# A transformer block on one core: four orders of instructions, and the square of the hidden layer in one VectorE instruction

## The chip, the cores and the metric

The kernel runs on one core of one Trainium2 chip. A core has TensorE (PE; its weight loads are PEld), VectorE (DVE), ScalarE (ACT), GpSimd (POOL), and SyncE (SP), which here issues nearly all DMAs. The metric is the device time of one execution in microseconds (us), the median over runs. The profile is one execution seen by the hardware profiler.

## The reference

```python
def reference(x, norm1_g, w_in, sinks_a, rel_bias_b, out_norm_a_g, out_norm_b_g,
              w_out, norm2_g, w_ff1, w_ff2, final_norm_g):
    n = rms_norm(x, norm1_g)                       # x: 1024 rows x 1024
    qa, ka, va, qb, kb, vb = split(n @ w_in)       # 64 per head
    ya = mixer_a(qa, ka, va, sinks_a)              # 8 heads, 2 of keys; window, ALiBi, sinks
    yb = mixer_b(qb, kb, vb, rel_bias_b)           # 8 heads; own chunk of 64 and 8 before
    y = concat(rms_norm(ya, out_norm_a_g), rms_norm(yb, out_norm_b_g))
    h = x + y @ w_out
    n = rms_norm(h, norm2_g)
    u = square(relu(n @ w_ff1))                    # 1024 x 4096
    h = h + u @ w_ff2
    return rms_norm(h, final_norm_g)
```

Everything is float32, and the kernel keeps about that accuracy.

## The kernel before

Every matrix is used as a sum of a high and a low part, and a product is three matmuls (high by high, high by low, low by high; `mm3`). A split is two instructions: ScalarE rounds to the high part, and VectorE or GpSimd subtracts it from the whole for the low part (`split` at L1395 and L1397 or L1399; `split_y` at L914 and L917 for the attention's outputs).

The first 430 us hold the input projection, the two attentions and the output projection. Matmuls of the projections are filled in between those of the attention. The names the change touches: `values_b` copies one half of the last value projection `vB3` out of its PSUM bank into `ts_vB` (L433), and at the second half takes its maximum (L438). `UnitB.end` joins two parts of a head's output into `Y` (L907, L908). `split_ya` splits a quarter `y` of group A's outputs, which `load_ya` (L947) reads back from DRAM. `out_proj_a` multiplies the quarters q = 0 to 3 with the weights, for each block `tb` of 128 rows and each half `dh` of the 1024 columns, into a bank `op_A`; ScalarE evacuates it to `o` (L1064) and GpSimd adds it to `h`. The row maximum of the scores `S_B` is taken in L620 and L622.

The MLP's products are made by a Strassen scheme of seven products of half size. In ff1 a column group n = 0 to 7 (512 columns of `w_ff1`) runs the products p = 1, 5, 6, 3, 7, 2, 4. Their left operands `X` come from n by transposes (`turned`) and sums (`second_half` for the blocks 1,1 and 1,0: `F` on ScalarE, L1301, and `S` on VectorE, L1304 and L1305; `combined`, `operand`). The right ones, `W`, come from four weight blocks `w`, which ScalarE scales by a power of two found from their maximum (`scaled1`, L1362), then sums `T` on VectorE (L1369), then the split. `product1` runs the matmuls `f`, and evacuates a bank to `kept[p]` (L1447, p = 1, 5, 6) or adds a bank to what is kept and takes the maximum (L1457, p = 3, 7, 2). ScalarE then rectifies with the scale `down1[n]` and squares (L1458, L1459), and `put` stores u in DRAM as `ud`. After p = 4 four more sums on VectorE give the other operands. Also in ff1, `look2` loads each block of `w_ff2` as `m` (512 KB), and ScalarE squares it with a sum (`see_squares`, L1176), from which the scale of that block's group follows.

In ff2, `fetch2` loads a `u` back, `prepare2` scales it by `uup[g]` and splits it to `U` (L1393 to L1399), forms the weight operand `Z` and splits it to `V`; `product2` runs the matmuls (`f_a`, `f_b`, `f_c`), and `add_up` adds them to `C` (L1711).

A framework orders each engine's instructions by a simulated schedule and places the semaphores. TensorE's order is kept as written. A `NoSync` dependency (`add_manual_dep`) orders two instructions of one engine without a wait, and `InOrder` keeps the DMAs of SP in the order in which they were put in. So the order of VectorE and ScalarE can move at places that the diff doesn't name.

Of the kernel before, what the change touches and what calls it, by code (L numbers as in the profile page):

```python
# [53 lines left out]
PAD = 32  # L54
# [4 lines left out]
def kernel(  # L59
# [364 lines left out]

    def values_b(acc, name, dst, t):
# [7 lines left out]
        nc.vector.tensor_tensor(st[:, t], acc, R1[:, t * HALF : (t + 1) * HALF], ALU.mult)  # L433
# [603 lines left out]
    def out_proj_a():  # L1037
# [6 lines left out]
        for tb in range(TB):  # L1044
# [6 lines left out]
            for n in range(8):  # L1051
                q, dh = (n // 2, n % 2) if tb == 0 else (n % 4, n // 4)
# [242 lines left out]
    def second_half(n, g):  # L1295

        if g not in S:
            F[2, g] = page([P, 2, HALF], f"F2{g}", F32)
# [2 lines left out]
        nc.scalar.activation(a22, turned(1, 1, n, g), AF.Copy)  # L1301
# [3 lines left out]
        dve.tensor_tensor(s3, a11, a21, ALU.subtract)  # L1305
# [40 lines left out]
    def scale1(n):  # L1346
# [3 lines left out]
        down1[n] = power(scale_tile("down1", str(n), 3), e, 1.0, -W_UP)  # L1350
# [3 lines left out]
    to_scale1 = {}  # L1354

    def scaled1(n, *blocks):
        up1, left = to_scale1[n]
        for b in blocks:
            if b in left:
                left.remove(b)  # L1360
                w = w1s[(n, *b)]
                nc.scalar.activation(w, w, AF.Copy, scale=up1)  # L1362
# [26 lines left out]
    def split(full, name, engine, alloc, up=None):  # L1389
# [5 lines left out]
        nc.scalar.activation(w[0], full, AF.Copy, scale=1.0 if up is None else up)  # L1395
# [24 lines left out]
    def product1(n, p):  # L1420
# [32 lines left out]
        if p == 4:  # L1453
            nc.scalar.activation(v, ps, AF.Relu, scale=down1[n])
            dve.tensor_reduce(top, ps, mybir.AxisListType.X, ALU.max)
        else:
# [1 line left out]
            nc.scalar.activation(v, v, AF.Relu, scale=down1[n])  # L1458
        nc.scalar.activation(v, v, AF.Square)  # L1459
# [17 lines left out]
        nc.vector.tensor_tensor(col, col, down1.pop(n), ALU.mult)  # L1477
# [117 lines left out]
    def scale_of_u(g, spread=True):  # L1595
# [3 lines left out]
        uup[g] = power(scale_tile("uup", str(g), 4), e, -2.0, 381 + U_UP)  # L1599
# [14 lines left out]
    def prepare2(at):  # L1614
        if at >= len(order2) or order2[at][1:] in ready2:
# [9 lines left out]
            split(a, f"U{n}_{p}", dve if p == 5 else pool, high, uup[g]), split(b, f"V{n}_{p}", dve, high, up2[g])  # L1625
# [42 lines left out]
    for i in range(LOAD2 - 2, LOAD2):  # L1668
# [249 lines left out]
```

## Time and profile before

| | us |
|---|---|
| median of 3 runs | 1038.84 (1038.01 to 1040.87) |
| the profiled execution | 1040.53 |
| its span in the profile | 1038.7 |
| busy in it: PE, DVE, ACT, POOL | 1000.8, 742.5, 692.6, 443.9 |

An engine's busy time is a share of the span; where it idles, the profile names the instruction that released it. TensorE's clock can be lowered; the profile gives the granted share. In rows of the timeline there stand the start, the length of the group, the engine, the source line, the operation, output and inputs, shape, count, and in brackets the idle time ahead of it with what ended it.

### The profile page before, as it was taken

Reading aid. Unit: us, or ns where it says so; the run is one execution under the profiler, and the core shown is the slowest. Engines: PE = TensorE matmul, PEld = TensorE weight load, DVE = VectorE, ACT = ScalarE, POOL = GpSimd, SP = SyncE. Lnnn points to the kernel's source line nnn. Section 1 sums busy time; section 2 is a strip of 40 time slices with the busy share of each in tenths; the row PEclk is TensorE's granted clock in tenths of the full one; section 3 lists DMA queues with packets and bytes.
Section 4 is the critical chain, followed back from the end, with each engine's and each line's share of the span. In section 5 each row is a group of like instructions: output and inputs, shape, how many; then the busy total and the mean of one; then the engine's idle time right before and its main releaser. Section 6 shows DMA issues by size and latency. Waiting matters only on the chain.

```text
span 1038.7 us, 14057 instructions
## 1 busy us (share of the span) xinstructions
PE 1000.8 (96%) x4818; PEld 591.8 (57%) x4818; DVE 742.5 (71%) x1259; ACT 692.6 (67%) x1102; POOL 443.9 (43%) x341
## 2 busy tenths in 40 slices
PE   9999999999979999899999999999899999999997
PEld 7878887777757678544444444444344444444443
DVE  6566777867586748994676667664798776786776
ACT  8666766667577736675867865964777765567346
POOL 0456665242453562105245425434255343345333
PEclk9999999999989999989999999999999999999999
DMA  9944438999999885105678668648699545433004
GB/s 353 254 133 133 129 82 184 194 209 225 209 257 251 207 261 182 62 21 166 211 282 293 205 210 274 195 170 310 257 329 388 189 150 186 159 121 122 1 1 162
DMA packets 150567, 200.63 MB, mean 193 GB/s; under 512 B 78688, under 2 KB 96224, under 8 KB 150496
## 3 DMA queue, kind: packets, MB, share of 16 engines
q1 hardware_dynamic: 150352, 199.47, 63.6%
q8 instruction: 38, 0.62, 0.3%
q14 instruction: 33, 0.27, 0.1%
q10 hardware_dynamic: 144, 0.26, 0.1%
HBM read 120.01 MB, written 42.99 MB: 157 GB/s over the span
## 4 chain that ended last, share of the span: by engine, by line
PE 34%; ACT 8%; issue 7%; DMA 7%; DVE 6%; POOL 2%; SPq 1%; DVEq 0%; POOLq 0%; ACTq 0%
PE f_a L171 13%; PE f_c L171 7%; PE f L171 6%; PE f_b L171 4%; DMA w<-in_w_ff_dram 3%; PE op_B L171 2%; ACT w L1362 2%; DMA m<-in_w_ff_dram 2%; DMA u<-ud 2%; POOL W L1397 2%; ACT k L1459 1%; ACT k L1458 1%; ACT W L1395 1%; DMA G_B<-H_B 1%; ACT m L1176 1%
## 5 line engine op out<-in xcount | busy, mean ns | idle before, releaser
L171 PE MATMUL f<-X,W 128*128 128x512 f16 x1344 | 295.3, 381 | 6.6 <-POOL W L1397 5.0
L171 PEld LDWEIGHTS <-U 128*128 128x128 f16 x1356 | 133.0, 98 | 163.9 <-issue 7.2
L171 PEld LDWEIGHTS <-W 128*128 128x128 f16 x1344 | 131.4, 98 | 166.3 <-POOL W L1397 8.2
L1397 POOL TENSOR_TENSOR U<-u,U 128x1024 f16<-128x1024 f32 x48 | 117.3, 2454 | 170.5 <-ACT U L1395 155.2
L171 PE MATMUL f_a<-V,U 128*128 128x512 f16 x756 | 165.3, 379 | 1.0 <-DVE C L1711 1.0
L1397 POOL TENSOR_TENSOR W<-T,W 128x1024 f16<-128x1024 f32 x29 | 69.7, 2407 | 84.3 <-ACT W L1395 84.3
L1397 POOL TENSOR_TENSOR W<-w,W 128x1024 f16<-128x1024 f32 x21 | 51.6, 2458 | 98.6 <-ACT W L1395 98.6
L171 PE MATMUL f_c<-V,U 128*128 128x512 f16 x384 | 86.0, 384 | 3.5 <-DVE V L1399 2.2
L1393 ACT ACTIVATE u<-u,uup 128x1024 f32<-128x1024 f32 x48 | 53.9, 1141 | 53.1 <-DMA u<-ud 53.0
L1399 DVE SCALAR_TENSOR_TENSOR V<-Z,up,V 128x1024 f16<-128x1024 f32 x32 | 51.3, 1605 | 28.7 <-ACT V L1395 20.7
L1395 ACT ACTIVATE U<-u 128x1024 f16<-128x1024 f32 x48 | 50.2, 1046 | 28.1 <-DVE Z L1369 10.4
L623 ACT ACTIVATE P_B<-P_B,nm_B 128x640 f32<-128x640 f32 (+2 forms) x64 | 44.2, 691 | 32.2 <-DVE nm_B L620 16.6
L171 PE MATMUL op_A<-w_o,y 128*128 128x512 f32 x192 | 58.0, 428 | 4.1 <-DVE ts_vB L433 3.9
L868 DVE SCALAR_TENSOR_TENSOR H_B<-P_B,rc_B,H_B 128x640 f16<-128x640 f32 (+2 forms) x64 | 51.0, 825 | 13.6 <-ACT H_B L863 13.3
L1399 DVE SCALAR_TENSOR_TENSOR V<-w,up,V 128x1024 f16<-128x1024 f32 x24 | 42.2, 1756 | 18.0 <-ACT V L1395 13.8
L171 PE MATMUL ip_qB<-nT,w_qB 128*128 128x512 f32 x192 | 53.7, 406 | 1.1 <-DVE t_kB L407 1.0
L171 PE MATMUL ip_kB<-nT,w_kB 128*128 128x512 f32 x192 | 53.7, 405 | 0.0
L1457 DVE CUSTOM_DVE_ANT_0 k<-f,k 128x1024 f32<-128x1024 f32 x24 | 29.3, 1220 | 31.3 <-PE f L171 22.4
L171 PE MATMUL ip_vB<-nT,w_vB 128*128 128x512 f32 x192 | 51.3, 400 | 0.0
L1395 ACT ACTIVATE V<-Z,up 128x1024 f16<-128x1024 f32 x32 | 36.4, 1138 | 22.2 <-DVE Z L1369 19.3
L171 PE MATMUL ip_qA<-nT,w_qA 128*128 128x512 f32 x192 | 50.7, 398 | 0.3 <-DVE VA L177 0.3
L863 ACT ACTIVATE H_B<-P_B,rc_B 128x640 f16<-128x640 f32 (+2 forms) x64 | 40.8, 685 | 9.5 <-DVE rc_B L860 4.2
(284 smaller groups left out, 1980.1 us busy)
## 6 DMA issues: line engine op xcount, KB each, us to landing
w<-in_w_ff_dram SPq DMA_DIRECT2D x64, 512.0 KB, 7.5
u<-ud SPq DMA_DIRECT2D x56, 512.0 KB, 5.4
ud<-k SPq DMA_DIRECT2D x48, 512.0 KB, 3.1
m<-in_w_ff_dram SPq DMA_DIRECT2D x32, 512.0 KB, 5.8
KkB<-t_kB SPq DMA_DIRECT2D x32, 256.0 KB, 5.0
xr<-in_x_dram SPq DMA_DIRECT2D x8, 512.0 KB, 8.8
st_o<-in_w_out_dram SPq DMA_DIRECT2D x8, 512.0 KB, 4.8
h<-in_x_dram SPq DMA_DIRECT2D x8, 512.0 KB, 4.9
```

The lines of the kernel that those rows point to most:

```text
L171: pe(nc.tensor.matmul(*args, **kw))
L623: nc.scalar.activation(pr, pr, AF.Exp, bias=nm, scale=-1.0, accum_out=sm)
L863: nc.scalar.activation(hi, q, AF.Copy, scale=rc)
L868: nc.vector.scalar_tensor_tensor(lo, q, rc, hi, ALU.mult, ALU.subtract)
L1176: nc.scalar.activation(src, src, AF.Square, accum_out=self.column())
L1362: nc.scalar.activation(w, w, AF.Copy, scale=up1)
L1393: nc.scalar.activation(full, full, AF.Copy, scale=up)
L1395: nc.scalar.activation(w[0], full, AF.Copy, scale=1.0 if up is None else up)
L1397: engine.tensor_tensor(w[1], full, w[0], ALU.subtract)
L1399: engine.scalar_tensor_tensor(w[1], full, up, w[0], ALU.mult, ALU.subtract)
L1457: dve.tensor_tensor_reduce(v, ps, v, 1.0, 0.0, ALU.add, ALU.max, top)
L1458: nc.scalar.activation(v, v, AF.Relu, scale=down1[n])
```

## The change

1. `FIRST_BLOCK`: in `out_proj_a`, the first block of rows alternates the two column halves of the quarters 0 and 1.
2. `behind_values`: the low parts of y and the sum in `UnitB.end` are ordered behind the copy of `vB3`'s second half on VectorE, once that is made.
3. `second_half` is cut in two steps, and between the transposes of `F` and of `S` six matmuls are put.
4. `last_w`: a scale of a weight block is ordered behind the last high part that was split.
5. For p = 3, 7 and 2, VectorE rectifies and squares in one instruction, max(v, 0) times v, in place of ScalarE's two; the scale `down1[n]` no longer enters there. For p = 4 ScalarE keeps both, without the scale. Instead `uup` is now made for each n, as the scale of the group times `down1[n]` squared, and enters where u is split in ff2.
6. `look2` starts one product earlier and leaves out other loads; from `fetch2` one u more is loaded in the last group at p = 6; four operands instead of two are prepared in ff1.
7. `PAD` and the pool of `all` move tiles in SBUF.

```diff
+FIRST_BLOCK = ((0, 0), (1, 0), (0, 1), (1, 1), (2, 0), (2, 1), (3, 0), (3, 1))
-PAD = 32
+PAD = 96
...
+    def behind_values(ins):
+        if freed:
+            dep = mybir.DependencyInfo(mybir.DependencyClass.NoSync, mybir.DependencyReason.DATA)
+            tc.add_manual_dep(ins.ins, freed[0], dep, reason="program order")
...
-        nc.vector.tensor_tensor(st[:, t], acc, R1[:, t * HALF : (t + 1) * HALF], ALU.mult)
+        ins = nc.vector.tensor_tensor(st[:, t], acc, R1[:, t * HALF : (t + 1) * HALF], ALU.mult)
+        if (name, t) == ("vB3", 1):
+            freed.append(ins.ins.name)
...
-            nc.vector.tensor_tensor(y, self.av[:HD], y, ALU.add)
+            behind_values(nc.vector.tensor_tensor(y, self.av[:HD], y, ALU.add))
...
-        split_y(y, f(y[:, 1]), ogc[:, m : m + 1])
+        behind_values(split_y(y, f(y[:, 1]), ogc[:, m : m + 1]))
...
-                q, dh = (n // 2, n % 2) if tb == 0 else (n % 4, n // 4)
+                q, dh = FIRST_BLOCK[n] if tb == 0 else (n % 4, n // 4)
...
-            self.all = small.tile([P, P], F32, tag="all", bufs=1, name=f"all_{self.name}")
+            self.all = fp.tile([P, P], F32, tag="all", bufs=1, name=f"all_{self.name}")
...
-                nc.scalar.activation(w, w, AF.Copy, scale=up1)
+                ins = nc.scalar.activation(w, w, AF.Copy, scale=up1)
+                if last_w:
+                    dep = mybir.DependencyInfo(mybir.DependencyClass.NoSync, mybir.DependencyReason.DATA)
+                    tc.add_manual_dep(ins.ins, last_w[0], dep, reason="program order")
...
-        nc.scalar.activation(w[0], full, AF.Copy, scale=1.0 if up is None else up)
+        last_w[:] = [nc.scalar.activation(w[0], full, AF.Copy, scale=1.0 if up is None else up).ins.name]
...
-            nc.scalar.activation(v, ps, AF.Relu, scale=down1[n])
+            nc.scalar.activation(v, ps, AF.Relu)
+            nc.scalar.activation(v, v, AF.Square)
...
-            nc.scalar.activation(v, v, AF.Relu, scale=down1[n])
-        nc.scalar.activation(v, v, AF.Square)
+            dve.scalar_tensor_tensor(v, v, 0.0, v, ALU.max, ALU.mult)
...
-        steps((second_half, 1, g))
-        steps()
+        steps((last_part, 1, g))
+        steps((third_part, 1, g))
...
-        uup[g] = power(scale_tile("uup", str(g), 4), e, -2.0, 381 + U_UP)
+        up = power(scale_tile("uup", str(g), 2), e, -2.0, 381 + U_UP)
+        for n in range(g * GQ, (g + 1) * GQ):
+            uup[n] = scale_tile("uupn", str(n), NQ)
+            down = down1.pop(n)
+            nc.vector.tensor_scalar(uup[n], up, down, down, ALU.mult, ALU.mult)
...
-        if at > 7:
-            look2(at, p != 1)
+        if at > 6:
+            look2(at, n < 2 or p not in (1, 5))
...
-                for i in range(LOAD2 - 2):
+                for i in range(LOAD2 - 1):
                     fetch2(i)
-            if p in (7, 2):
-                prepare2({7: 0, 2: 1}[p])
+            for i in {7: (0,), 2: (1, 2, 3)}.get(p, ()):
+                prepare2(i)
```

VectorE's order where `vB3`'s second half is copied (H_B are attention weights, P_B and nm_B the scores and their negative row maximum), before:

```order
L917 SCALAR_TENSOR_TENSOR y_2_3405<-y_2_3405,ogc 128x512
L868 SCALAR_TENSOR_TENSOR H_B_1_1_3490<-P_B_1_0_3458,rc_B_1_3455,H_B_1_1_3490 128x640
L868 SCALAR_TENSOR_TENSOR H_B_1_1_3490<-P_B_1_1_3482,rc_B_1_3455,H_B_1_1_3490 128x640
L620 ISA P_B_1_3_3538,nm_B_1_3453<-S_B_1_3_3537,b_B_587 128x640
L620 ISA nm_B_1_3453 128x1
L917 SCALAR_TENSOR_TENSOR y_3_3407<-y_3_3407,ogc 128x512
L908 TENSOR_TENSOR Y_0_3472<-av_B_0_3494,Y_0_3472 64x512
L433 TENSOR_TENSOR ts_vB_3399<-ip_vB_1_3548,R_180 128x512
L622 ISA P_B_0_0_3612,nm_B_0_3607<-S_B_0_0_3611,b_B_586 128x128
```

and now:

```order
L879 SCALAR_TENSOR_TENSOR H_B_1_1_3490<-P_B_1_0_3458,rc_B_1_3455,H_B_1_1_3490 128x640
L879 SCALAR_TENSOR_TENSOR H_B_1_1_3490<-P_B_1_1_3482,rc_B_1_3455,H_B_1_1_3490 128x640
L631 ISA P_B_1_3_3538,nm_B_1_3453<-S_B_1_3_3537,b_B_587 128x640
L631 ISA nm_B_1_3453 128x1
L442 TENSOR_TENSOR ts_vB_3399<-ip_vB_1_3548,R_180 128x512
L928 SCALAR_TENSOR_TENSOR y_2_3405<-y_2_3405,ogc 128x512
L919 TENSOR_TENSOR Y_0_3472<-av_B_0_3494,Y_0_3472 64x512
L928 SCALAR_TENSOR_TENSOR y_3_3407<-y_3_3407,ogc 128x512
L449 TENSOR_REDUCE top_vB_3580<-ts_vB_3399 128x1
L633 ISA P_B_0_0_3612,nm_B_0_3607<-S_B_0_0_3611,b_B_586 128x128
```

The copy has moved ahead of y_2, y_3 and the sum Y, and these with the maximum top_vB stand ahead of the next row maximum.

ScalarE's order some 20 us later (o_1 is the evacuation of op_A_1, y_0 and y_1 the first splits of the second half's quarter), before:

```order
L623 ACTIVATE P_B_0_1_3764,sm_B_0_3737<-P_B_0_1_3764,nm_B_0_3736 128x256
L1064 ACTIVATE o_1_3776<-op_A_1_3756,rgA 128x512
L623 ACTIVATE P_B_0_2_3783,sm_B_0_3737<-P_B_0_2_3783,nm_B_0_3736 128x384
L863 ACTIVATE H_B_0_1_3769<-P_B_0_0_3741,rc_B_0_3738 128x128
L863 ACTIVATE H_B_0_1_3769<-P_B_0_1_3764,rc_B_0_3738 128x256
L623 ACTIVATE P_B_0_3_3811,sm_B_0_3737<-P_B_0_3_3811,nm_B_0_3736 128x512
L914 ACTIVATE y_0_3704<-y_0_3704,ogc 128x512
L1064 ACTIVATE o_0_3827<-op_A_0_3797,rgA 128x512
L914 ACTIVATE y_1_3706<-y_1_3706,ogc 128x512
```

and now:

```order
L634 ACTIVATE P_B_0_1_3764,sm_B_0_3737<-P_B_0_1_3764,nm_B_0_3736 128x256
L634 ACTIVATE P_B_0_2_3783,sm_B_0_3737<-P_B_0_2_3783,nm_B_0_3736 128x384
L874 ACTIVATE H_B_0_1_3769<-P_B_0_0_3741,rc_B_0_3738 128x128
L874 ACTIVATE H_B_0_1_3769<-P_B_0_1_3764,rc_B_0_3738 128x256
L925 ACTIVATE y_0_3704<-y_0_3704,ogc 128x512
L925 ACTIVATE y_1_3706<-y_1_3706,ogc 128x512
L1076 ACTIVATE o_1_3776<-op_A_1_3756,rgA 128x512
L634 ACTIVATE P_B_0_3_3811,sm_B_0_3737<-P_B_0_3_3811,nm_B_0_3736 128x512
```

The evacuation o_1 has moved behind y_0 and y_1.

ScalarE's order ahead of the first split of group 5 in ff1 (w_5_.. are the weight blocks of the group, m_.. the blocks of w_ff2), before:

```order
L1176 ACTIVATE m_5_00_6185,tops_w_2_6084<-m_5_00_6185 128x1024
L1458 ACTIVATE k_6_6117<-k_6_6117,down_4_5917 128x1024
L1459 ACTIVATE k_6_6117<-k_6_6117 128x1024
L1458 ACTIVATE k_5_6082<-k_5_6082,down_4_5917 128x1024
L1362 ACTIVATE w_5_00_6006<-w_5_00_6006,up_5_6227 128x1024
L1362 ACTIVATE w_5_01_6008<-w_5_01_6008,up_5_6227 128x1024
L1362 ACTIVATE w_5_11_6012<-w_5_11_6012,up_5_6227 128x1024
L1362 ACTIVATE w_5_10_6010<-w_5_10_6010,up_5_6227 128x1024
L1459 ACTIVATE k_5_6082<-k_5_6082 128x1024
L1176 ACTIVATE m_5_01_6233,tops_w_2_6084<-m_5_01_6233 128x1024
L1395 ACTIVATE W_1_6237<-w_5_00_6006 128x1024
```

and now:

```order
L1188 ACTIVATE m_4_01_6107,tops_w_2_6105<-m_4_01_6107 128x1024
L1188 ACTIVATE m_4_11_6175,tops_w_2_6105<-m_4_11_6175 128x1024
L1188 ACTIVATE m_4_10_6221,tops_w_2_6105<-m_4_10_6221 128x1024
L1381 ACTIVATE w_5_00_5995<-w_5_00_5995,up_5_6216 128x1024
L1381 ACTIVATE w_5_01_5997<-w_5_01_5997,up_5_6216 128x1024
L1417 ACTIVATE W_1_6225<-w_5_00_5995 128x1024
L1381 ACTIVATE w_5_11_6001<-w_5_11_6001,up_5_6216 128x1024
L1188 ACTIVATE m_5_00_6257,tops_w_2_6105<-m_5_00_6257 128x1024
L1417 ACTIVATE W_5_6262<-T_5_6260 128x1024
```

The rectify and square instructions are gone from it, two scales have moved behind the split of W_1, and the block m_4_10 has moved up to it.

More of the change, by code (lines that the diff above doesn't have):

```diff
@@ L423, in keys_b @@
                         nc.sync.dma_start(f(dst[2 * hl + s][rep * HD : (rep + 1) * HD]), src)
+    freed = []
+    def behind_values(ins):
+        if freed:
+            dep = mybir.DependencyInfo(mybir.DependencyClass.NoSync, mybir.DependencyReason.DATA)
+            tc.add_manual_dep(ins.ins, freed[0], dep, reason="program order")
     def values_b(acc, name, dst, t):
@@ L1295, in second_half, with last_part @@
     def second_half(n, g):
+        last_part(n, g)
+        third_part(n, g)
+    def last_part(n, g):
         if g not in S:
@@ L1299, in second_half, with third_part @@
             S[g] = [(page if g else page2)([P, 2, HALF], f"S{i}_{g}", F32) for i in range(4)]
+        nc.scalar.activation(F[2, g][:, :, part(n)], turned(1, 1, n, g), AF.Copy)
+    def third_part(n, g):
         a11, _, a22 = (F[d, g][:, :, part(n)] for d in range(3))
-        nc.scalar.activation(a22, turned(1, 1, n, g), AF.Copy)
         a21 = turned(1, 0, n, g)
@@ L1349, in scale1 @@
         up1 = power(scale_tile("up1", str(n), 2), e, -1.0, 254 + W_UP)
-        down1[n] = power(scale_tile("down1", str(n), 3), e, 1.0, -W_UP)
+        down1[n] = power(scale_tile("down1", str(n), 5), e, 1.0, -W_UP)
         nc.vector.tensor_tensor(down1[n], down1[n], xdown, ALU.mult)
         to_scale1[n] = up1, [(0, 0), (0, 1), (1, 1), (1, 0)]
-    to_scale1 = {}
+    to_scale1, last_w = {}, []
     def scaled1(n, *blocks):
@@ L1476, in product1 @@
         nc.vector.tensor_reduce(col, top, mybir.AxisListType.X, ALU.max)
-        nc.vector.tensor_tensor(col, col, down1.pop(n), ALU.mult)
+        nc.vector.tensor_tensor(col, col, down1[n], ALU.mult)
         if n % GQ == GQ - 1:
@@ L1624, in prepare2 @@
         ops2[n, p] = (
-            split(a, f"U{n}_{p}", dve if p == 5 else pool, high, uup[g]), split(b, f"V{n}_{p}", dve, high, up2[g])
+            split(a, f"U{n}_{p}", dve if p == 5 else pool, high, uup[n]), split(b, f"V{n}_{p}", dve, high, up2[g])
         )
@@ L1666, in load_acc @@
             queue[0].dma_start(acc[i, j, n], hB[2 * i + n][:, :, j * HALF : (j + 1) * HALF])
-    for i in range(LOAD2 - 2, LOAD2):
+    for i in range(LOAD2 - 1, LOAD2):
         fetch2(i)
```

## The prediction

> **What bounds the kernel now.** I read the first part of the page, then TensorE's table of waits, a table of stretches, and the timeline around each wait.
>
> ```profile
> PE 1000.8 (96%) x4818; PEld 591.8 (57%) x4818; DVE 742.5 (71%) x1259; ACT 692.6 (67%) x1102; POOL 443.9 (43%) x341
> ```
>
> TensorE is busy for 1000.8 of 1038.7 us, and the change takes no matmul away. So at most the 37.9 us in which TensorE idles can be won, and what it loses at a lowered clock. The waits (us in total, times, longest) that concern the change are these:
>
> ```profile
> PE f L171 <- POOL W L1397: 5.0, 4, 1.6
> PE op_A L171 <- DVE ts_vB L433: 3.9, 1, 3.9
> PE S_B L171 <- DVE nm_B L620: 3.7, 4, 1.7
> PE f_c L171 <- DVE V L1399: 2.2, 1, 2.2
> PE tp L174 <- ACT F L1301: 2.0, 1, 2.0
> PE tp L174 <- DVE S L1305: 1.9, 1, 1.9
> PE f L171 <- ACT W L1395: 1.5, 2, 0.8
> PE f_c L171 <- ACT V L1395: 1.2, 1, 1.2
> ...
> 300.00:312.00 12.00, 8.09 (x29) 6.08 (x28) 10.27 (x23) 9.14 (x18) 8.97 (x13) 0.72 1.04 271
> 440.00:450.00 10.00, 8.06 (x30) 3.74 (x29) 10.00 (x16) 5.30 (x8) 0.00 (x0) 0.66 0.00 1
> 575.00:625.00 50.00, 46.70 (x218) 20.91 (x216) 31.59 (x50) 39.08 (x47) 21.07 (x9) 1.00 0.65 213
> 747.00:755.00 8.00, 5.34 (x17) 1.99 (x17) 8.00 (x7) 4.55 (x5) 2.17 (x1) 0.79 1.03 408
> 755.00:1000.00 245.00, 245.00 (x1137) 111.06 (x1136) 189.00 (x140) 149.78 (x144) 106.42 (x43) 1.00 0.49 171
> ```
>
> The stretches give busy us of PE, PEld, DVE, ACT and POOL, then the granted clock. Four places stand out, each the target of one edit: A (300 to 312), B (440 to 450), C (the start of a new column group in ff1, clock 1.00) and D (747 to 755). At A, B and D the clock falls below 1, so a wait there costs more than its own length. From 755 on TensorE never pauses, so an earlier start at D moves the end one for one.
>
> **Place A: the values copy, and what is then behind it.**
>
> ```profile
> 302.54 0.84 DVE L917 SCALAR_TENSOR_TENSOR y<-y,ogc 128x512 fp32r<-128x512 f32 x1
> 304.38 0.69 DVE L433 TENSOR_TENSOR ts_vB<-ip_vB,R 128x512 f32<-128x512 f32 x1
> 305.13 2.93 PE L171 MATMUL op_A<-w_o,y 128*128 128x512 f32 x6 [3.92 <-DVE ts_vB L433]
> ...
> 322.75 0.67 ACT L1064 ACTIVATE o<-op_A,rgA 128x512 f32<-128x512 f32 x1
> 323.27 2.33 SPq L947 DMA_DIRECT2D y<-ya  x4
> 327.26 1.05 PE L171 MATMUL op_A<-w_o,y 128*128 128x512 f32 x3
> 328.58 0.72 ACT L914 ACTIVATE y<-y,ogc 128x512 fp32r<-128x512 f32 x1 [0.93 <-DMA y<-ya]
> ```
>
> TensorE waits 3.92 us for the copy that empties the bank of vB3, and its next six matmuls take 2.93 us where three at 327.26 take 1.05: another 0.8 us, and by the mean clock of 0.72 more after them; I call it 1.4, in all 5.3. With the new order the copy takes the place of the first y behind the row maximum L620, so it runs from 302.54 to 303.24 instead of 304.38 to 305.07, 1.8 us earlier, and FIRST_BLOCK puts three matmuls that don't need that bank (1.05) ahead of those that do. That alone would leave a wait of 3.92-1.83-1.05 = 1.0 us at full clock, a gain of about 4.3. But two low parts y (0.84 each), the sum Y and the reduction of the copied tile are now ahead of the row maxima L622 that release the next two score blocks; DVE has only 12.00-10.27 = 1.7 us free there. I take about 1.4 us as what TensorE keeps.
>
> The order of after shows a new wait behind it. ScalarE's evacuation o_1 (322.75, 0.67) now stands behind y_0 and y_1 of the next quarter, which wait for their load: 323.27 to 328.58, 5.3 us from issue. The load goes out earlier by about the 1 us that TensorE and its queue gain, so y_0 and y_1 end near 327.6+2x0.72 = 329.0, and o_1 at 329.7 instead of 323.42. TensorE needs that bank at 327.26 less 1.4 = 325.9: a wait of 3.8, about as long as the one that was removed, and likely to lower the clock as that one did (half of 2.4 is taken). Of it, about 1.3 us of the longest later wait of the scores on L620 (1.7 of its 3.7 us) is filled. Sum for A: -1.4+3.8+1.2-1.3 = **+2.3**; bounds -5.3 (all goes, nothing comes) and +6.2 (nothing kept, all of the new wait and 2.4 of clock).
>
> **Place B: transposes of block 1,1.**
>
> ```profile
> 430.00 4.27 ACT L1362 ACTIVATE w<-w,up 128x1024 f32<-128x1024 f32 x4 [0.60 <-DVE up L1154]
> 439.78 0.66 PE L174 MATMUL tp<-ident,n 128*128 128x128 f32 x4 [1.98 <-ACT F L1301]
> 442.37 1.09 PE L174 MATMUL tp<-ident,n 128*128 128x128 f32 x4 [1.94 <-DVE S L1305]
> 443.25 8.94 PE L171 MATMUL f<-X,W 128*128 128x512 f16 x31
> ```
>
> Two waits, 1.98+1.94; the transposes behind the second take 1.09 instead of 0.66, and 31 matmuls 8.94 us where 103 take 22.41 (a row below), 0.288 each against 0.218: 2.2. In all 6.5. The new order of the scales takes two of the four L1362 (half of 4.27) from ahead of the evacuation F, so the first wait goes; the twelve matmuls put between the transposes cover some of the second. But DVE is busy for 10.00 of 10.00 us here, and gets the first new square (about 1.3) ahead of the low part of the operand X_4815 that the seventh next product needs. Counting DVE's rows through in the new order, that operand is ready about 1.3 us earlier than now, where a full cover would need 6.5. I take **-1.3**; bounds -5.0 and +0.9 (the square beside a POOL instruction, below).
>
> **Place C: ScalarE's queue in ff1.** Group 5 stands for groups 2 to 6:
>
> ```profile
> 614.43 4.25 ACT L1362 ACTIVATE w<-w,up 128x1024 f32<-128x1024 f32 x4
> 619.54 1.04 ACT L1176 ACTIVATE m<-m 128x1024 f32<-128x1024 f32 x1
> 620.58 1.04 ACT L1395 ACTIVATE W<-w 128x1024 f16<-128x1024 f32 x1
> 621.69 2.12 POOL L1397 TENSOR_TENSOR W<-w,W 128x1024 f16<-128x1024 f32 x1 [13.02 <-ACT W L1395]
> 623.87 22.41 PE L171 MATMUL f<-X,W 128*128 128x512 f16 x103 [1.60 <-POOL W L1397]
> ...
> m<-in_w_ff_dram SPq DMA_DIRECT2D x32, 512.0 KB, 5.8
>   DMA m<-in_w_ff_dram: 12.7, 13
> ...
> L1458 ACT ACTIVATE k<-k,down x24: 1132/1134/1149, 449.4 to 735.2; 128x1024 f32<-128x1024 f32 x24
> L1459 ACT ACTIVATE k<-k x24: 1039/1045/1058, 450.6 to 736.3; 128x1024 f32<-128x1024 f32 x24
> L1256 DVE SCALAR_TENSOR_TENSOR n<-h,r_n,g2b x8: 1283/1284/2160, 391.3 to 430.1; 128x1024 f32<-128x1024 f32 x8
> ```
>
> The first product of a group waits for the high and low part of W_1, 0.8 and 1.6 us each time; over the phase 5.0+1.5 = 6.5. ScalarE runs four scales, a square and an m sum before the split. The change removes 24 x 1.134 + 24 x 1.045 = 52.3 us from ScalarE, and puts two of the scales behind the split. Then the split needs only m, two scales and itself. But m is loaded (5.8 us), and SP issues that load behind a store of u which now follows VectorE's new instruction; 13 of the 32 m sums already wait for their load, 12.7 us. With the load landing near 614.6 the high part ends at 614.6+1.04+2x1.06+1.04 = 618.8 instead of 621.6, and POOL's part at 620.9 instead of 623.8: 2.9 earlier, more than the 2.4 of waits, with 0.5 to spare. For group 2 the same count, with an estimate of 504.3 for its load, gives a wait about 1.3 longer than the 0.9 of now (part of the 1.5 in the table). Sum: -(6.5-0.9)+1.3 = **-4.3**; bounds -6.5 and 0.
>
> VectorE gets 24 instructions over 1024 elements, the nearest of which took 1.28 (L1256) and at most 2.16: 31 to 52 us, less 0 on the path, since in 575 to 625 it was busy for 31.59 of 50 and gets some 6 more. The eight small scale products stand in that slack too. Merging down twice into the scale of U changes a scalar operand alone.
>
> One price hangs on the neighbour:
>
> ```profile
> 734.29 2.14 POOL L1397 TENSOR_TENSOR U<-u,U 128x1024 f16<-128x1024 f32 x1 [1.84 <-ACT U L1395]
> 735.35 2.17 DVE L1399 SCALAR_TENSOR_TENSOR V<-w,up,V 128x1024 f16<-128x1024 f32 x1 [0.67 <-issue]
> ```
>
> An instruction of that kind that starts during a POOL instruction runs on until 1.09 us after its end, 0.9 longer than the 1.28 above. With POOL busy for 21.07 of 50 us, that costs the 24 squares about 10 us of VectorE's slack, and nothing of the path while the low part of W_1 has its 0.5 us. The Trainium skill, SBUF — State Buffer, section "SBUF: two separate sides", says that VectorE with two SBUF inputs and GpSimd take turns on a shared port pair, whoever starts first keeping it for the whole instruction, which speaks against moving a square onto VectorE, since v is both of its inputs. By that rule a square could also hold back POOL's split of W_1 by its full 1.28 us; at five groups, less the 0.5 to spare, the sum below would be up to 3.9 higher. The row agrees for VectorE; no row shows POOL held.
>
> **Place D: the first u of ff2.**
>
> ```profile
> 737.78 1.25 SPq L152 DMA_DIRECT2D u<-ud  x2
> 744.14 1.15 ACT L1393 ACTIVATE u<-u,uup 128x1024 f32<-128x1024 f32 x1 [4.67 <-DMA u<-ud]
> 750.04 7.24 PE L171 MATMUL f_c<-V,U 128*128 128x512 f16 x25 [2.24 <-DVE V L1399]
> ```
>
> Waits of 1.2+2.24, and 25 matmuls at 0.290 instead of 0.218: 1.8. In all 5.2. The second of the two loads goes out some 19 us earlier (at p=6, ahead of the last group's stores), and the V operands are prepared a product earlier (1, 2, 3 at p=2), so both waits go. What is late next is the accumulator C and V_6, about 0.8. **-4.5**; bounds -5.2 and -2.
>
> **Elsewhere.** PAD moves tiles in memory alone, and the tile all changes pool; nothing waits for either in the rows above, and TensorE's order differs only at A, at the transposes and at three small ones. 0.
>
> **Sum.** +2.3-1.3-4.3-4.5 = -7.8. The profiled execution took 1040.53, 1.7 above the median of 1038.84, so 1032.7 for one like it and **1031** for the median.
>
> **Rivals.**
> 1. Every wait goes, and nothing takes its place: 5.3+6.5+6.5+5.2 = 23.5, so 1015. For it: the four edits hit the four places with a lowered clock or repeated waits. Against: o_1 behind a load at A, and DVE's 10.00 of 10.00 at B. With one of A and B it would be about 1023. Together 0.17.
> 2. No change, 1038 to 1041: A at its upper bound (+6.2), B at +0.9, and C and D at -3 and -4. For it: the new wait at A. 0.15.
> 3. Slower: the m load sets C. At each of the seven new groups W_1's high part on ScalarE is behind an m sum, whose load SP issues behind a store that waits for VectorE. If loads land 3.7 us later than I count, each of seven groups waits 3.7-0.5 = 3.2 us, 22 us where 6.5 stood, so C is +16 and the time 1051; from 2 us later on (7 x 1.5 = 10.5, C +4.0) with the rest as forecast the time is 1039, and from 2.5 us on (14, C +7.5) it is 1043, slower by over 0.3%. For it: 13 waits for such loads now, and fewer other instructions ahead to hide them. Against: median landing of 5.8, no DMA of ff1 above it, 0.65 of DMA share. 0.10.
>
> **Chances.** 0.3% of this time, 3.1 us, is about what a measurement can tell from no change. My forecast, 1024 to 1035.7, has 0.58; it, with rival 1, gives faster 0.75, rival 2 same 0.15, rival 3 slower 0.10. The range goes from between rival 1's two times, 1019, to 1039.5, past most of rival 2: that leaves out about 0.08 below and 0.12 above.
>
> **What would show it.** A: ts_vB right behind L620, no wait near 305 above 1.6 us, but an op_A at about 326 waiting 3 to 4 us for ACT's o; if not, A is -4 and I am too high. B: no wait at 439.8, one of 2 to 3 us for X about 8 us later. C: no f waiting for W from group 3 on; one of about 2.2 at group 2; ScalarE waiting for m. VectorE's squares between 1.28 and 2.2. D: no wait of f_c at 747; a C wait under 1.5. Wrong would be a long wait for W in each group, or a TensorE pause after 755.

## The result, and the profile after

| | before | after |
|---|---|---|
| median of 4 runs each | 1039.47 (1038.01 to 1040.87) | 1055.85 (1054.87 to 1057.68) |
| the profiled execution, its span | 1040.53, 1038.7 | 1057.68, 1055.9 |

The changed kernel takes 1.0158 times the time before [1.0145, 1.0172], 16.4 us more. The prediction had 1031 with a range up to 1039.5: its sign was wrong. Two executions of the kernel before, measured beside `e5` to `e8` below, ran at a granted clock of 0.75 and 0.65 and took 1276 and 1670 us; they are left out of the medians and ratios.

The first part of the page of after (the profile of the changed kernel):

```profile
PE 1002.7 (95%) x4818; PEld 591.7 (56%) x4818; DVE 795.5 (75%) x1291; ACT 644.7 (61%) x1054; POOL 448.0 (42%) x341
```

TensorE's work has hardly grown (1002.7 against 1000.8), so 15.3 of the 17.2 us by which the span grew are idle time. VectorE gained 53 us of work and ScalarE lost 48, near what was counted (31 to 52, and 52). TensorE's table of waits of after (us in total, times, longest):

```profile
PE f L172 <- POOL W L1419: 5.8, 6, 1.9
PE f_c L172 <- ACT U L1417: 4.7, 1, 4.7
PE op_A L172 <- ACT o L1076: 4.0, 1, 4.0
...
PE f_a L172 <- DVE topf L1480: 2.6, 1, 2.6
PE f_c L172 <- DVE C L1737: 2.4, 1, 2.4
PE f L172 <- ACT W L1417: 2.3, 2, 1.8
```

The waits for W were to vanish and are longer (5.8+2.3 against 5.0+1.5). New are one for o (forecast) and those of 4.7, 2.6 and 2.4 at and behind the start of ff2 (not forecast).

Where the time was lost is best read from the start of the same matmul in two traces, counted through TensorE's order. The lag is after minus before, in us. In ff2 the 756 matmuls f_a are counted:

| up to | lag | place's own part | forecast |
|---|---|---|---|
| the end of the attention (A) | +3.0 | +3.0 | +2.3 |
| the end of the transposes (B) | +1.7 | -1.3 | -1.3 |
| ahead of column group 7 | -0.05 | -1.75 | |
| the first matmul of ff2 | +5.2 | +5.25 (with the row above C: +3.5) | C: -4.3 |
| f_a matmul 150, at 815.7; lost by 785 (D) | +11.1 | +5.9 | -4.5 |
| f_a matmul 755, the last; lost at 993 | +15.3 | +4.2 | 0 |
| the end of the span | +17.2 | +1.9 | 0 |

**A and B** came by the mechanism worked out. The timeline of after at A:

```profile
303.98 1.65 PE L172 MATMUL op_A<-w_o,y 128*128 128x512 f32 x3 [2.26 <-DVE ts_vB L442]
...
329.23 0.72 ACT L925 ACTIVATE y<-y,ogc 128x512 fp32r<-128x512 f32 x1 [3.86 <-DMA y<-ya]
330.82 0.67 ACT L1076 ACTIVATE o<-op_A,rgA 128x512 f32<-128x512 f32 x1
331.55 1.65 PE L172 MATMUL op_A<-w_o,y 128*128 128x512 f32 x3 [4.04 <-ACT o L1076]
```

The wait for ts_vB fell from 3.92 to 2.26, and o, now behind a y that waits 3.86 for its load, makes a new one of 4.04; 3.8 was forecast. At B the wait for F is gone, that for S stays, and the forecast one for X has come:

```profile
455.06 5.12 PE L172 MATMUL f<-X,W 128*128 128x512 f16 x23 [2.69 <-DVE X L1297]
```

**C.** ScalarE and TensorE of after ahead of group 5, against the rows of before from 614.43 on:

```profile
613.63 1.06 ACT L1188 ACTIVATE m<-m 128x1024 f32<-128x1024 f32 x1 [3.41 <-DMA m<-in_w_ff_dram]
614.91 1.06 ACT L1188 ACTIVATE m<-m 128x1024 f32<-128x1024 f32 x1
618.93 1.06 ACT L1188 ACTIVATE m<-m 128x1024 f32<-128x1024 f32 x1 [2.87 <-DMA m<-in_w_ff_dram]
619.99 2.17 ACT L1381 ACTIVATE w<-w,up 128x1024 f32<-128x1024 f32 x2
622.07 1.04 ACT L1417 ACTIVATE W<-w 128x1024 f16<-128x1024 f32 x1
...
625.47 9.88 PE L172 MATMUL f<-X,W 128*128 128x512 f16 x45 [1.25 <-POOL W L1419]
```

Three m sums stand ahead of the scales, and the third waits for its load until 618.93; I had it at 614.6. The high part ends at 623.1 instead of the counted 618.8. ScalarE is idle for loads most of that time: over the phase its waits for m (from the view of the m line) grew from 12.7 us in 13 to this:

```profile
  DMA m<-in_w_ff_dram: 39.2, 12
```

Group 5 still starts with no longer a wait than before (1.25 against 1.60); group 7 does not. The timeline there:

```profile
687.28 2.12 POOL L1419 TENSOR_TENSOR W<-T,W 128x1024 f16<-128x1024 f32 x1 [5.90 <-ACT W L1417]
687.32 3.17 DVE L1481 SCALAR_TENSOR_TENSOR k<-k 128x1024 f32<-128x1024 f32 x1
690.52 0.34 SPq L153 DMA_DIRECT2D ud<-k  x1
690.95 1.17 SPq L153 DMA_DIRECT2D m<-in_w_ff_dram  x1
696.70 1.06 ACT L1188 ACTIVATE m<-m 128x1024 f32<-128x1024 f32 x1 [4.51 <-DMA m<-in_w_ff_dram]
697.75 2.17 ACT L1381 ACTIVATE w<-w,up 128x1024 f32<-128x1024 f32 x2
699.83 1.04 ACT L1417 ACTIVATE W<-w 128x1024 f16<-128x1024 f32 x1
700.93 0.60 PE L172 MATMUL f<-X,W 128*128 128x512 f16 x2 [1.78 <-ACT W L1417]
```

Read upwards from TensorE's wait: W is behind two scales, these behind an m sum, that behind a load, the load in SP's queue behind a store of u, and the store behind VectorE's new square, which took 3.17 us since it began 0.04 us after POOL's split. That is rival 3's chain. Behind this wait come one of 1.69 for POOL's low part of W_1 and matmuls at a lowered clock (0.92 from 690 to 706).

**D.** The start of ff2 in after:

```profile
717.01 5.92 SPq L153 DMA_DIRECT2D w<-in_w_ff_dram  x8
...
729.75 20.32 SPq L153 DMA_DIRECT2D ud<-k  x3
735.04 1.15 ACT L1415 ACTIVATE u<-u,uupn 128x1024 f32<-128x1024 f32 x1 [12.84 <-DMA u<-ud]
738.41 2.15 DVE L1421 SCALAR_TENSOR_TENSOR V<-w,up,V 128x1024 f16<-128x1024 f32 x1 [5.19 <-issue]
...
744.92 1.21 DVE L1480 CUSTOM_DVE_ANT_0 k<-f,k 128x1024 f32<-128x1024 f32 x1
746.19 7.93 PE L172 MATMUL f_a<-V,U 128*128 128x512 f16 x36 [2.58 <-DVE topf L1480]
748.51 1.21 DVE L1481 SCALAR_TENSOR_TENSOR k<-k 128x1024 f32<-128x1024 f32 x1
750.16 0.38 SPq L153 DMA_DIRECT2D u<-ud  x1
...
781.61 8.75 PE L172 MATMUL f_c<-V,U 128*128 128x512 f16 x32 [4.67 <-ACT U L1417]
```

The two waits of before ahead of f_c (1.24 and 2.24) are down to one of 0.50, as forecast, but new ones have come. The first u lands 18.0 us after SP began to issue eight weight blocks ahead of it (717.01 to 735.04). ScalarE waits 12.84 us; behind u stand VectorE's splits and Z sums of the operands prepared ahead, behind these the evacuation of p = 2 (744.92, TensorE waits 2.58), the last square (748.51) and its store, and behind the store, in SP's order, the next load of u (750.16). Later operands are late with it, up to the 4.67 at 781.61, whose u SP issued at 767.26, behind the last stores of ff1.

### The profile page after: what moved, and what is told of

It is laid out like the page before. It is cut to its first block, busy times and chain, and to the rows that moved or that the text cites. A ratio compares the mean times of both kernels' runs of the same rounds, so it can differ in the third digit from the quotient of the medians.

```text
span 1055.9 us, 14037 instructions
## 1 busy us (share of the span) xinstructions
PE 1002.7 (95%) x4818; PEld 591.7 (56%) x4818; DVE 795.5 (75%) x1291; ACT 644.7 (61%) x1054; POOL 448.0 (42%) x341
## 5 line engine op out<-in xcount | busy, mean ns | idle before, releaser
L1419 POOL TENSOR_TENSOR W<-T,W 128x1024 f16<-128x1024 f32 x29 | 75.5, 2606 | 95.5 <-ACT W L1417 95.5
L1415 ACT ACTIVATE u<-u,uupn 128x1024 f32<-128x1024 f32 x48 | 54.4, 1144 | 73.1 <-DMA u<-ud 72.8
L1419 POOL TENSOR_TENSOR W<-w,W 128x1024 f16<-128x1024 f32 x21 | 48.9, 2328 | 86.6 <-ACT W L1417 86.6
L634 ACT ACTIVATE P_B<-P_B,nm_B 128x640 f32<-128x640 f32 (+2 forms) x64 | 44.2, 690 | 31.8 <-DVE nm_B L631 16.4
L1417 ACT ACTIVATE W<-T 128x1024 f16<-128x1024 f32 x29 | 30.5, 1050 | 48.1 <-DVE T L1391 48.1
L1188 ACT ACTIVATE m<-m 128x1024 f32<-128x1024 f32 x32 | 33.6, 1049 | 39.8 <-DMA m<-in_w_ff_dram 39.2
```

The source lines that it names most:

```text
L634: nc.scalar.activation(pr, pr, AF.Exp, bias=nm, scale=-1.0, accum_out=sm)
L1188: nc.scalar.activation(src, src, AF.Square, accum_out=self.column())
L1415: nc.scalar.activation(full, full, AF.Copy, scale=up)
L1417: last_w[:] = [nc.scalar.activation(w[0], full, AF.Copy, scale=1.0 if up is None else up).ins.name]
L1419: engine.tensor_tensor(w[1], full, w[0], ALU.subtract)
```

## The experiments

Each median stands beside that of the kernel before, measured with it; a ratio is to that kernel, and those medians of the kernel before range from 1039.47 to 1042.51. Lags are from one profiled execution each.

### Taking parts out of the changed kernel

The first theory was that most is lost by the loads and operands put ahead in the last group (edit 6); its rival, that the squares on VectorE cost it by way of ScalarE's order. `e1_no_ahead` undoes `fetch2` and `prepare2` of edit 6:

```diff
-                for i in range(LOAD2 - 1):
+                for i in range(LOAD2 - 2):
                     fetch2(i)
-            for i in {7: (0,), 2: (1, 2, 3)}.get(p, ()):
-                prepare2(i)
+            if p in (7, 2):
+                prepare2({7: 0, 2: 1}[p])
```

> The changed kernel with the first operands of ff2 as before: three u loaded at p = 6 and two operands made in ff1, all other edits kept. In the changed trace TensorE loses 5.9 us between 740 and 782 (f_a waits 2.6 for topf, f_c 4.7 for U), 4.2 near 993 and about 2 after it, 12 in all. Theory 1: this comes from preparing four operands in ff1, whose sums and splits stand on VectorE ahead of the evacuation of p = 2 and of the last square, behind which SP holds the next loads of u. Then it is 12 us faster than the changed kernel, about 1044. Theory 2: it comes from the squares on VectorE, which delay the stores that SP issues in order. Then it stays at 1052 to 1056. The wait near 993 tells whether the lag of ff2 starts here: gone by theory 1.

Measured: 1050.15 against 1040.10, 1.0084 [1.0056, 1.0111]. Half of the loss stays. The lag at the start of ff2 is still +4.2, at matmul 150 +6.5, and at 755 +6.5: nothing is lost at 993 any more.

`e2_no_square` gives rectify and square back to ScalarE (edit 5 undone, `uup` by group again):

```diff
             dve.tensor_tensor_reduce(v, ps, v, 1.0, 0.0, ALU.add, ALU.max, top)
-            dve.scalar_tensor_tensor(v, v, 0.0, v, ALU.max, ALU.mult)
+            nc.scalar.activation(v, v, AF.Relu, scale=down1[n])
+        nc.scalar.activation(v, v, AF.Square)
```

> The changed kernel with rectify and square on ScalarE as before (scale in the rectify, one scale of u per pair of groups), all other edits kept. Theory 1 (the operands prepared ahead cost the 12 us): the 3.5 us lost in ff1 go, perhaps some more, the rest stays: 1049 to 1053. Theory 2 (VectorE's squares cost both): 1038 to 1042. In ff1 theory 1 expects the long VectorE instructions of 3.2 us (a square that meets a GpSimd split) to be gone, and no wait for W over 1 us at group 7.

Measured: 1046.74, 1.0054 [1.0039, 1.0069], between the two. ScalarE's waits for m fall to 18.6 us, and the lag at the start of ff2 to +0.4; D still loses 4.9. So neither theory holds all.

`e3_no_attention` leaves out `FIRST_BLOCK` and `behind_values`:

```diff
-                q, dh = FIRST_BLOCK[n] if tb == 0 else (n % 4, n // 4)
+                q, dh = (n // 2, n % 2) if tb == 0 else (n % 4, n // 4)
...
-        behind_values(split_y(y, f(y[:, 1]), ogc[:, m : m + 1]))
+        split_y(y, f(y[:, 1]), ogc[:, m : m + 1])
```

> The changed kernel without the edits in the attention (first block order and the order behind the values copy), all other edits kept. By the changed trace TensorE is 3.0 us late at the end of the attention, from a wait of 4.0 us for ScalarE's o, so this should be 3 us faster than the changed kernel, about 1052.8. If the later stages absorb the lag (their waits are on loads that don't move with it), nothing: 1055.8.

Measured: 1053.13, 1.0120 [1.0090, 1.0150], 2.7 below the changed kernel by the medians and 4.0 by the ratios, whose intervals touch. The traces agree: between 298 us and the end of the attention the eight builds with both edits lose 3.2 to 5.7 us against before, and the seven with the old order -0.3 to +0.7. So A costs somewhat more than forecast.

### Parts alone on the kernel before

`e4_transposes` has edits 3 and 4 alone, `e5_square_alone` edit 5 alone:

```diff
-        steps((second_half, 1, g))
-        steps()
+        steps((last_part, 1, g))
+        steps((third_part, 1, g))
...
+                if last_w:
...
+                    tc.add_manual_dep(ins.ins, last_w[0], dep, reason="program order")
```

> The kernel before with two edits alone: the cut of the second half's steps at the transposes, and the scales of weight blocks behind the last split. Theory: 1.3 us less at the transposes as in the changed trace (a wait of 1.9 and one of about 2.7 for X stay), and between 2 and 4 us less at the starts of groups, where the scales of two blocks leave the queue ahead of W: 1034 to 1036. Rival: the start of a group is set by VectorE's sum or by the sums over the blocks of w_ff2, then 1038.

Measured: 1039.19, 0.9981 [0.9965, 0.9998], missed by the theory and near the rival's 1038, though not by its cause: at the start of ff2 it is 5.0 us ahead (3.8 of it from C, near the 4.3 forecast there), and at matmul 150 0.4 behind:

```profile
706.92 6.33 SPq L152 DMA_DIRECT2D w<-in_w_ff_dram  x8
725.36 1.15 ACT L1403 ACTIVATE u<-u,uup 128x1024 f32<-128x1024 f32 x1 [6.41 <-DMA u<-ud]
```

The first u lands 18.4 us after the weights' first issue here too (before: 710.29 to 727.11, 16.8). The start of ff2 hangs on that transfer, so what ff1 gains is given back.

> The kernel before with one edit: rectify and square on VectorE, with the scale of u for each n. Theory 1: the square on VectorE costs by itself, since its end is the start of a store that SP issues in order, ahead of the loads for the weights' scales and of u; in the changed kernel taking it out gave 9 us. Then 1044 to 1049, and ScalarE's waits for m rise from 12.7 to 25 us or more. Theory 2: it costs only together with the new orders and loads: 1038 to 1041. Theory 3, that of the prediction: ScalarE's 52 us less shorten the starts of groups: 1033 to 1036.

Measured: 1048.51 against 1040.70, 1.0066 [1.0046, 1.0086]. One wait, ahead of group 2, shows how:

```profile
502.21 1.06 ACT L1176 ACTIVATE m<-m 128x1024 f32<-128x1024 f32 x1 [9.76 <-DMA m<-in_w_ff_dram]
503.26 4.25 ACT L1362 ACTIVATE w<-w,up 128x1024 f32<-128x1024 f32 x4
```

and so does ScalarE's idle time for m over the phase:

```profile
  DMA m<-in_w_ff_dram: 39.0, 17
```

With ScalarE's 48 instructions gone, m sums move up ahead of the weight scales, and those wait with them.

### The loads of m

`e6_loads_as_before` undoes the `look2` part of edit 6 in the changed kernel; `e8_m_ahead` calls it ahead of `product1`:

```diff
-        if at > 6:
-            look2(at, n < 2 or p not in (1, 5))
+        if at > 7:
+            look2(at, p != 1)
```

> The changed kernel with the loads of the blocks of w_ff2 (m) spread over the products as before. If the new spread makes the loads late (ScalarE waits 39.2 us for m in the changed kernel, 18.6 without the squares on VectorE and 12.7 before), those waits fall below 25 us, and 3 to 5 us come back at group 7: 1051 to 1053. If the squares and their stores make them late, the waits stay above 30 us and the time at 1054 to 1057.

Measured: 1061.32, 1.0181 [1.0132, 1.0230], above both expectations. ScalarE's waits for m stay at 38.3 us, so the new spread of the loads is not what makes them late; whether it saves anything is not shown (1.0181 against 1.0158, the intervals overlap).

```diff
+        if at > 6:
+            look2(at, n < 2 or p not in (1, 5))
         product1(n, p)
...
-        if at > 6:
-            look2(at, n < 2 or p not in (1, 5))
```

> The changed kernel with the load of each m issued one store earlier (the look at the blocks stands ahead of the product's evacuation, not behind it). Theory: SP issues in order, and the m loads are late since they stand behind stores of VectorE's squares. Then ScalarE's waits for m fall from 39.2 to under 25 us and 3 to 5 us come back in ff1: 1051 to 1053. Rival: the loads wait for their tile or for the DMA engines, then the waits stay and the time is 1055 to 1057.

Measured: 1074.23, 1.0315 [1.0286, 1.0343], a miss the other way. Each load was called for a store earlier, but a fourth m sum now stands ahead of the scales of group 6, where the changed kernel has three; the waits for m rose to 50.8 us, the one there to 7.49:

```profile
676.96 1.06 ACT L1188 ACTIVATE m<-m 128x1024 f32<-128x1024 f32 x1 [7.49 <-DMA m<-in_w_ff_dram]
```

That turned the question from when m is loaded to what stands behind its sum.

### The first u ahead of the weights

`e7_u_first` is `e4_transposes` with the first two loads of u ahead of the eight weight blocks; `e9_first_square` adds edit 5 to it (the diff of edit 5 as above):

```diff
+            if p == 1:
+                for i in range(2):
+                    fetch2(i)
             if p in (1, 5):
...
             if p == 6:
-                for i in range(LOAD2 - 2):
-                    fetch2(i)
+                fetch2(2)
```

> The kernel of the transposes' and scales' orders (e4) with one more edit: the first two u of ff2 are loaded ahead of the eight blocks of w_ff2, not behind them. In e4 TensorE was 5.0 us ahead of the kernel before at the start of ff2, and 0.4 behind it 20 us later. Theory: the first u lands 18 us after that burst of 4 MB began, ScalarE waits for it with the last squares behind it, SP holds the second u of p = 5 behind the store of those, and TensorE waits. Then with the u first ScalarE's wait for u is gone, f_c waits less than 2 us, and the 5 us or up to 10 stay: 1029 to 1034. Rival: the burst itself sets the start by its bytes, the operands for the first products are then late by the weights: 1037 to 1040.

Measured: 1032.67 against 1040.70, 0.9921 [0.9897, 0.9944], as expected. Both u are scaled long before they are needed:

```profile
704.27 1.31 SPq L152 DMA_DIRECT2D u<-ud  x2
...
709.57 1.15 ACT L1403 ACTIVATE u<-u,uup 128x1024 f32<-128x1024 f32 x1 [3.91 <-DMA u<-ud]
```

The u lands 5.3 us after its own issue, where behind the weights it took 11.1 (before) to 12.0 (after, e4) and was issued some 6 us later in the series. The lead at the start of ff2, 6.3, is 7.4 at matmul 150 and stays so to 755.

> e7 (orders of the transposes and scales, first u ahead) with one more edit: rectify and square on VectorE. With ScalarE emptied, the schedule puts two to four m sums ahead of the scales of each new group, where e7 has none that waits long. Theory: ScalarE takes its instructions in order, so those sums wait for their loads with the scales and W behind them; 4 to 8 us are lost at starts of groups, 1037 to 1041, and ScalarE's waits for m are above 30 us (10.9 in e7). Rival: the squares cost in VectorE's own time and on the port it shares with GpSimd: the same loss, but the next kernel tells.

Measured: 1052.94 against 1042.51, 1.0107 [1.0073, 1.0142]. The same edit that cost 7 us on the kernel before costs 20 here, well above the 4 to 8 expected. ScalarE and TensorE ahead of group 5 (the first and the last of four m sums):

```profile
613.15 1.06 ACT L1176 ACTIVATE m<-m 128x1024 f32<-128x1024 f32 x1 [3.76 <-DMA m<-in_w_ff_dram]
...
619.63 1.06 ACT L1176 ACTIVATE m<-m 128x1024 f32<-128x1024 f32 x1 [2.65 <-DMA m<-in_w_ff_dram]
620.68 2.17 ACT L1369 ACTIVATE w<-w,up 128x1024 f32<-128x1024 f32 x2
622.76 1.04 ACT L1405 ACTIVATE W<-w 128x1024 f16<-128x1024 f32 x1
...
626.15 9.02 PE L171 MATMUL f<-X,W 128*128 128x512 f16 x41 [1.69 <-POOL W L1407]
```

The lag is +6.1 at the start of group 7 and +13.1 at the start of ff2. So 7.0 us are lost in that group. There no m sum holds up W_1; the instruction that waits for a load is the scale of the first u, whose load SP issues behind late stores:

```profile
726.49 1.15 ACT L1403 ACTIVATE u<-u,uupn 128x1024 f32<-128x1024 f32 x1 [7.08 <-DMA u<-ud]
...
730.48 1.00 ACT L1457 ACTIVATE k<-f 128x1024 f32<-128x1024 f32 x1
```

The evacuation k stands behind it, and TensorE waits 3.77 us for k.

### The order of the m sums

The theory now: VectorE's squares cost little by themselves; what costs is the m sums put ahead of the scales and W_1. The rival: VectorE's late squares and the port that it shares with POOL. `e10_square_m_behind` is e9 with the m sums ordered behind the last split, and none called for at p = 7 ahead of the next group's W_1; no instruction is added or removed. `e11_m_behind` has the same order without edit 5:

```diff
-            nc.scalar.activation(src, src, AF.Square, accum_out=self.column())
+            ins = nc.scalar.activation(src, src, AF.Square, accum_out=self.column())
+            if last_w:
...
+                tc.add_manual_dep(ins.ins, last_w[0], dep, reason="program order")
...
-        if on_way and on_way[0][0] + 3 <= at:
+        while see and on_way and on_way[0][0] + 3 <= at:
...
-            look2(at, p != 1)
+            look2(at, p != 1, not 0 < n < NQ - 1 or p != 7)
```

> e9 with one more edit: each m sum is ordered behind the last split high part on ScalarE, and those of product 7 are made after the split of the next group's W_1. Squares stay on VectorE. Theory (m sums ahead of W): the loss of e9 goes, no wait for W over 1.9 us, 1031 to 1034. Rival (VectorE's time, the shared port): the time stays within 2 us of e9.

Measured: 1032.63, 0.9922 [0.9893, 0.9951]: 20.3 us less than e9 by the order of one kind of instruction. The same place:

```profile
609.75 2.19 ACT L1372 ACTIVATE w<-w,up 128x1024 f32<-128x1024 f32 x2 [7.37 <-DVE up L1154]
611.85 1.04 ACT L1408 ACTIVATE W<-w 128x1024 f16<-128x1024 f32 x1
612.79 1.04 ACT L1176 ACTIVATE m<-m 128x1024 f32<-128x1024 f32 x1
...
609.64 25.63 PE L171 MATMUL f<-X,W 128*128 128x512 f16 x118
```

W_1 is rounded 11 us earlier, no m waits, and TensorE runs through the start of the group. VectorE's squares are all still there and meet POOL as often: 10 of the 24 take over 1.5 us and all of them 44.7 us, in e9 10 and 44.6. So the rival falls for this build. In group 7 the first u lands 17.2 us after the group's start (21.4 in e9), and TensorE waits only 0.17 for k.

> e7 with the m sums ordered behind W as in e10, squares on ScalarE as before. Theory: in e7 few of these sums wait, so little is gained or lost: 1030 to 1034. With e10 it gives the price of the squares alone once the order is mended: by the theory under 2 us.

Measured: 1030.61, 0.9904 [0.9871, 0.9937], the fastest of the study. Against e10 the squares on VectorE cost 2.0 us, less than their intervals tell apart.

`e12_first_block` adds `FIRST_BLOCK` alone (first line of the diff of e3, reversed) to e7:

> e7 with the order of the first block of the output projection alone (three matmuls that don't need the bank of vB3 ahead), without the order behind the values copy on VectorE. In this schedule ScalarE's evacuation o_1 stays ahead of the splits y_0 and y_1, so the wait of 4.0 us that the changed kernel has at 331 should not come. Theory: TensorE's wait near 305 falls from 3.9 to 2.9 or less and the clock falls less: 1029.5 to 1032. Rival: the scores behind it take the microsecond back: 1032 to 1034.

Measured: 1034.93, 0.9933 [0.9908, 0.9958]: no gain over e7's 0.9921, and above what both its theory and its rival allowed.

### The whole change, mended

`e13_changed_m_behind` gives the changed kernel the order of the m sums, `e14_changed_u_first` the loads of u ahead of the weights, and `e15_changed_m_behind_no_ahead` is e13 with the edit of e1 (all diffs as above).

> The whole changed kernel with one edit: the m sums ordered behind the split of W (as in e10). Theory: ff1's starts of groups are clean, no wait for W over 1.9 us, TensorE reaches ff2 8 to 10 us earlier than in the changed kernel; a part is given back there, since the first u still comes behind the burst of weights: 1044 to 1050. If the late m sums explain all of the loss, 1038 to 1042; if little, 1053 or more.

Measured: 1044.82 against 1041.04, 1.0032 [1.0020, 1.0043]. Of 16.4 us some 12.6 are gone (16.4 less 3.8).

> The whole changed kernel with one edit: the first two u loaded ahead of the eight weight blocks of ff2 (as in e7). ff1 keeps its waits. Theory: the 5.9 us lost at the start of ff2, and the lag that costs 6 more near 993 and behind it, come from ScalarE's wait of 12.8 us for the first u: 1044 to 1049. Rival: they come from the operands prepared ahead on VectorE: 1053 to 1057.

Measured: 1053.51, 1.0118 [1.0094, 1.0141]; missed, only about 4 gained by the ratios. From the start of ff2 to matmul 755 only 0.3 is lost instead of 10.1, but group 7 loses more than in the changed kernel (lag +9.5 at the start of ff2, there +5.2). As in e9, the scale of the first u waits 7.15 us for its load ahead of the evacuation k, and TensorE waits 3.84 for k.

> e13 with the first operands of ff2 as before (three u loaded, two operands made in ff1). Against e13 it prices the operands prepared ahead once ff1 is mended. Theory: as in e1 against the changed kernel, 4 to 7 us faster than e13, so 1039 to 1045. Rival: the preparation only cost because it met the late u, then within 2 us of e13.

Measured: 1042.09, 1.0008 [0.9996, 1.0019], level with the kernel before. The operands prepared ahead cost 2.7 once the m sums are mended, between theory and rival; in the profiles all of it is behind the start of ff2 (lag at 755: +5.3 in e13, +0.5 here).

## Why the prediction was wrong

- **A, right in sign and mechanism, too small.** +2.3 forecast, +3.0 in the lag, 4.0 by e3's ratio, at the place given: o behind y. The copy's wait kept 2.26 us, where none above 1.6 was expected.
- **B, right.** -1.3 forecast and measured, with the wait of 2 to 3 us for X that was expected (2.69, some 5 us later than said).
- **C, the step that failed: "With the load landing near 614.6".** It took ScalarE's queue from the order and its times from the trace of before. The load's issue depends on VectorE's square through a store in SP's queue, and not one m sum but three stand ahead of the scales: the load of the third landed at 618.9, 4.3 us later than counted. Forecast -4.3, measured +3.5; without the squares on VectorE, C gave -3.8 (e4). Rival 3 had this chain, at 0.10, as slower by all seven groups; here group 2 lost 1.6 and group 7 5.25, and groups 3 to 6 gained 3.35 between them. Its argument against ("median landing of 5.8, no DMA of ff1 above it") misread the trace, where the w loads of ff1 took 7.9 in the median, and looked at the transfer, not at when it is issued. e10 shows that the place of the m sums makes e9's loss, part of it by way of u in group 7, and e13 that it makes most of after's.
- **D, the step that failed: "What is late next is the accumulator C and V_6, about 0.8".** Both waits ahead of f_c went as forecast, but later ones of 2.58 (for the evacuation of p = 2) and 4.67 (for U) took their place. The u stand in SP's queue behind eight blocks of 512 KB, and the first landed 18.0 us after the first of these was issued (16.8 before, where ScalarE had squares to make in that time). The operands prepared earlier put waiting instructions on ScalarE and VectorE ahead of the end of ff1, for which I had no row and no price. Forecast -4.5, measured +5.9; with the first u ahead of the weights D loses nothing on either kernel (e7, and e14 with 0.3 to matmul 755).
- **The term "Elsewhere", 0, wrong by 6.1.** The accumulator C, a term of 0.8 in D, was late at 993, which cost 4.2 with the lowered clock behind it (0.89 from 985 to 1000):

```profile
989.46 2.21 DVE L1421 SCALAR_TENSOR_TENSOR V<-Z,up,V 128x1024 f16<-128x1024 f32 x1 [1.08 <-ACT V L1417]
991.59 2.46 DVE L1737 SCALAR_TENSOR_TENSOR C<-f_b,down,C 128x1024 f32<-128x1024 f32 x2
```

  The operands of ff2 ran late from D on and TensorE met them here. "From 755 on TensorE never pauses" held for an earlier start, not for late operands. The loss at 993 is gone in e1 and e15, which prepare two operands, and in e14, which prepares four but loads the first u ahead: so it takes both the preparing and the late u. How the lateness lasts 200 us was not taken apart. The other 1.9 lie behind the last matmul: the issue of the last store of the output took 2.43 us instead of 0.37. It took over 2 us in e1, e3, e9 and e15 too and at most 0.53 in the other runs; why is not shown.
- **VectorE's price.** The squares' median was 1.22 (1.28 taken), at most 3.17 (2.2 taken). "No row shows POOL held" was wrong: the trace of before has one, missed there.

```profile
592.44 3.15 DVE L1467 TENSOR_TENSOR v<-k,v 128x1024 f32<-128x1024 f32 x1
594.54 3.04 POOL L1397 TENSOR_TENSOR W<-T,W 128x1024 f16<-128x1024 f32 x1
```

The squares of after, from the view of their line:

```profile
L1481 DVE SCALAR_TENSOR_TENSOR k<-k x24: 1207/1220/3169, 451.4 to 748.5; 128x1024 f32<-128x1024 f32 x24
```

  A split that starts while VectorE's instruction runs took 3.04 instead of 2.12. The rule of the Trainium skill, SBUF — State Buffer, section "SBUF: two separate sides", that whoever starts first keeps the shared ports, agrees with the trace on both sides. By e10 and e11 the squares on VectorE cost 2.0 us in all once the queues are in order, which the intervals do not tell from nothing, and it was not what made the time.

What stays open: why the schedule moves the m sums up was read from the order alone; and no run puts the first u ahead and the m sums behind in the changed kernel, so the 3.8 us that e13 leaves are priced only in parts (A, the late u, the operands prepared ahead).

## What to carry to other kernels

Taking instructions off an engine that isn't the bound also moves what is left on it: before counting a gain, look in its new order for an instruction that waits for a load and now stands ahead of one that the bound needs (20 us here), and follow that load back through its issuing queue. An earlier call for a load is worth nothing if it is issued behind a burst; put the one that is needed first ahead (6 us by the ratios of e4 and e7), and see that what waits for it does not stand ahead of an evacuation (e9, e14). Price a move on the kernel it will stand in: the same edit cost 7 us alone, 20 on a faster kernel, and 2, which may be nothing, with the queue mended.

## What the hardware showed that was not expected

VectorE with two SBUF inputs and POOL wait out each other's instruction, in both directions: VectorE's 1.21 becomes 3.17 when it starts 0.04 us behind POOL's split, and POOL's 2.12 becomes 3.04 when it starts during VectorE's. And of twelve 512 KB loads issued within 12 us the ninth landed 18.0 us after the first issue and 12.0 after its own (after), where the first of such a series landed 5.3 us after its own (e7).
